# Score matmuls of a gated linear recurrence: from blocks of 64 keys in one or two column groups to blocks of 32 keys in four

## The chip, the cores and the metric

The kernel runs on one core of a Trainium2 chip as one program. The metric is the device time of one execution in microseconds (us), the median over several runs. Engines are named as in the profile: PE is TensorE (its matmuls) and PEld the loading of weights into TensorE; DVE is VectorE, ACT is ScalarE, POOL is GpSimd, SP is the engine whose queue issues nearly all DMAs.

## The reference

The program is a two-layer network in float32 on 1024 tokens of width 1024: sliding-window attention, a squared-relu MLP, a gated linear recurrence (HGRN2), and a second MLP. The change touches the recurrence alone. For each of its 8 heads (key and value width 128), in 16 chunks of 64 tokens, it computes

```python
b = jnp.cumsum(lc, axis=2)                       # lc = log of the forget gate
o_inter = jnp.einsum('bhtd,bhde->bhte', qc * jnp.exp(b), state)
diff = b[:, :, :, None, :] - b[:, :, None, :, :]
decay = jnp.exp(jnp.where(causal[None, None, :, :, None], diff, -jnp.inf))
scores = jnp.einsum('bhtd,bhtsd,bhsd->bhts', qc, decay, kc)
o_intra = jnp.einsum('bhts,bhse->bhte', scores, vc)
b_last = b[:, :, -1]
new_state = jnp.exp(b_last)[..., None] * state + jnp.einsum(
    'bhsd,bhse->bhde', kc * jnp.exp(b_last[:, :, None, :] - b), vc)
```

A score of a query at time t and a key at time s is thus a sum over 128 dimensions of q, k and the product of the forget gates between s and t. That product depends on the dimension, so the scores are not one matrix product.

## The kernel before, in words

**Layout.** Activations lie transposed: 128 dimensions on the partitions, 512 tokens (one half, `hf`) along a tile; `NH = 2` halves, `BPH = 4` blocks of 128 tokens in each. The kernel works the recurrence in blocks of 128 tokens.

**Scores by doubling.** For each head, `recurrence` builds the decayed queries and keys by doubling the span (`double`, H = 1, 2, 4 ... 64): at level `lg` (H = 2 to the power lg) the tokens are seen in spans of 2H; the queries of the later half of each span carry the gates' product back to the middle of the span, and the keys of the earlier half carry it on to there, so a plain matrix product gives the scores between the two halves of each span. `level` makes these products. Its weights are the keys, its moving columns the later halves of the queries alone (`later`), so half as many columns as keys. Of each product only the entries of the right spans are kept: `merge` copies them from PSUM into `scores` through a mask (COPY_PREDICATED on DVE). The diagonal comes from one more set of products (`own`), which DVE multiplies by `diag`.

**What is issued per head.** A chunk is `CH = 64` tokens; there are 16 in the two halves. Keys of even chunks write PSUM rows 0 to 63, keys of odd chunks rows 64 to 127; the PSUM rows are the column group of the TensorE array, so neighbours in the order go to different groups. `own` and the six levels 0 to 5 have 16 matmuls each; the products between the two chunks of a block of 128 tokens (`cross`) are 8 matmuls, all in rows 0 to 63. That makes 120 matmuls per head. They are float32, and the profile has two weight loads and two MATMUL records for each. They stand in two stretches: `own` and levels 0 to 2 first, levels 3 to 5 and `cross` some 16 us later, after further doublings.

**From scores to outputs.** ACT copies `scores` and `cross` into the 128 by 128 lower triangle `s` of every block (three copies for each half, 64 partitions by 256), POOL clears the upper corner, and later matmuls multiply `s` by the values and add the state's part.

**What sets the order.** No loop order is final. Each operation is recorded with a price per engine (`mm`, `tt`, `copy` and so on); `Schedule.order` simulates the engines with these prices in four passes of forward list scheduling and backward due times, and the best pass sets the order on every engine for the entire program. The recurrence of head e is woven into the gate projections of head e + 1 (`interleave` in `hgrn`): big matmuls of 128 by 512 against weights that ACT and DVE split into a high and a low part (`weight_split`: tiles `wh`, `wl`). All operations are issued by one helper, so the profile shows them all at one line; tiles tell them apart: `p` and `q` are PSUM banks (4 each), `t` and `a` float32 tiles, `wr` raw weights, `m` short-lived tiles, `c` constants, `d` DRAM. The score matmuls write `q`.

**Prices of the planner.** A score matmul is priced at 64 x 2.06 / 2.4 + 4 = 58.9 ns, one of `cross` at 64 x 3.9 / 2.4 + 4 = 108 ns; these numbers set an order, they are not measurements of this run.

Of the kernel before, what the change touches and what calls it, by code (L numbers as in the profile page):

```python
# [22 lines left out]
TH = T // NH  # L23
# [11 lines left out]
BPH = NBLK // NH  # L35
# [4 lines left out]
PI_DOWN = float(np.float32(3.1415925))  # L40
BUFS = {"a": 60, "t": 18, "m": 6, "sm": 8, "wr": 6, "wh": 5, "wl": 5, "p": 4, "q": 4}
CH = 64
LEVELS = 6
HOMES = "aaaaaaaaaaaa"
K_SPANS = ((-1, 3), (2, 6), (5, 8))

# [91 lines left out]
HALF = {"ACT": 125.0, "DVE": 105.0}  # L138
# [240 lines left out]
class Net:  # L379
# [1011 lines left out]
    def hgrn_constants(self):  # L1391
        bounds = self.const((P, 2 * KT))
        self.dma(bounds, self.io["lb"], 4 * P * 2 * KT)
        l0, l1 = (bounds[:, i * KT : i * KT + KT] for i in range(2))
        top, e0, e1, lb = (self.const((P, KT)) for _ in range(4))
        self.tt("DVE", top, l0, l1, ALU.max, KT)
        for e, l in ((e0, l0), (e1, l1)):
            self.tt("DVE", e, l, top, ALU.subtract, KT)
            self.act(e, e, AF.Exp, KT)
        self.tt("DVE", lb, e0, e1, ALU.add, KT)  # L1400
        self.op("DVE", self.nc.vector.reciprocal, [lb], [lb], 100, lb, lb)
        self.tt("DVE", e0, e0, lb, ALU.mult, KT)
        self.tt("DVE", e1, e1, lb, ALU.mult, KT)
        self.tt("DVE", lb, e0, e1, ALU.add, KT)
        self.tt("DVE", lb, lb, e0, ALU.subtract, KT)
        self.f_mul, self.f_add = self.const((P, KT)), self.const((P, KT))
        self.ts("DVE", self.f_mul, lb, -0.5, 0.5, ALU.mult, ALU.add, KT)
        self.tt("DVE", self.f_add, self.f_mul, lb, ALU.add, KT)
        nc = self.nc
        si, ti, bits = (self.t(I32, (P, CH)) for _ in range(3))  # L1410
        self.op("Pool", nc.gpsimd.iota, [si], [], 300, si, pattern=[[0, CH]], base=0, channel_multiplier=1)
        self.op("Pool", nc.gpsimd.iota, [ti], [], 300, ti, pattern=[[1, CH]], base=0, channel_multiplier=0)
        self.ts("DVE", si, si, CH - 1, None, ALU.bitwise_and, None, CH)
        self.tt("DVE", bits, si, ti, ALU.bitwise_xor, CH)
        self.diag = self.const((P, CH))
        self.ts("DVE", self.diag, bits, 0, None, ALU.is_equal, None, CH)
        self.level_mask = []
        for lg in range(LEVELS):
            mask, later = self.const((P, CH), I32), self.t(I32, (P, CH))
            self.ts("DVE", mask, bits, lg, None, ALU.logical_shift_right, None, CH)  # L1420
            self.ts("DVE", mask, mask, 1, None, ALU.is_equal, None, CH)
            self.ts("DVE", later, ti, 1 << lg, None, ALU.bitwise_and, None, CH)
            self.ts("DVE", later, later, 0, None, ALU.is_gt, None, CH)
            self.tt("DVE", mask, mask, later, ALU.mult, CH)
            self.level_mask.append(mask)

    def put_by(self, views):
# [85 lines left out]
    def recurrence(self, e, gates, totals, out):  # L1513

        nc = self.nc
        NC = NH * BPH
        chunk = lambda z, j: z[:, j * CH : j * CH + CH]
        scores = self.t(F32, (P, NC, CH))
        tots, tot = [self.t(tag="m") for _ in range(NH)], [g[1] for g in gates]
        qs, ks = ([g[i] for g in gates] for i in (0, 2))  # L1520
        later = lambda z, H: z.rearrange("p (n a h) -> p n a h", a=2, h=H)[:, :, 1]
        at = 0

        def level(lg, part, qs, ks, late):
            H = 1 << lg
            for hf, (q, k) in enumerate(zip(qs, ks)):
                for c in range(BPH):
                    for b in range(2):
                        rows, j = slice(b * CH, b * CH + CH), 2 * c + b
                        self.mm(part[rows, hf * BPH + c], chunk(k, j), later(chunk(q, j), H), True, True, CH, 2.06, "columns", late)  # L1530

        def merge(lg, part):
            H = 1 << lg
            n = CH // (2 * H)
            mask = later(self.level_mask[lg], H).unsqueeze(1).to_broadcast([P, NC, n, H])
            target = scores.rearrange("p c (n a h) -> p c n a h", a=2, h=H)[:, :, :, 1]
            part = part.rearrange("p c (n h) -> p c n h", n=n)
            self.op("DVE", nc.vector.copy_predicated, [target], [mask, part], 70 + TH // 2 * 1.04, target, mask, part)

        def part_of(bank, i):  # L1540
            return bank[:, i * TH // 2 : (i + 1) * TH // 2].rearrange("p (c t) -> p c t", c=NC)

        first = [self.t() for _ in range(NH)]
        for z, (q, f, k, g, v) in zip(first, gates):
# [2 lines left out]
        at, tot, q1, k1 = self.double(1, first, ks, tot, tots, at, self.t)  # L1547
        yield
        at, tot, q2, k2 = self.double(2, q1, k1, tot, tots, at, self.t)
        yield  # L1550
        own, low, two = (self.psum("q") for _ in range(3))
        own = own.rearrange("p (c t) -> p c t", c=NC)
        late = qs + ks + first + q1 + k1 + q2 + k2
        for hf, (q, k) in enumerate(zip(qs, ks)):
            for c in range(BPH):
                for b in range(2):
                    rows, j = slice(b * CH, b * CH + CH), 2 * c + b
                    self.mm(own[rows, hf * BPH + c], chunk(k, j), chunk(q, j), True, True, CH, 2.06, "columns", late)
        level(0, part_of(low, 0), first, ks, late)
        level(1, part_of(low, 1), q1, k1, late)  # L1560
        level(2, part_of(two, 0), q2, k2, late)
        self.tt("DVE", scores, own, self.diag.unsqueeze(1).to_broadcast([P, NC, CH]), ALU.mult)
        merge(0, part_of(low, 0))
        merge(1, part_of(low, 1))
        merge(2, part_of(two, 0))
        qs, ks = q2, k2
        yield
        at, tot, qs, ks = self.double(4, qs, ks, tot, tots, at)
        yield
        at, tot, q4, k4 = self.double(8, qs, ks, tot, tots, at, self.t)  # L1570
        yield
        at, tot, q5, k5 = self.double(16, q4, k4, tot, tots, at, self.a)
        yield
        at, tot, q6, k6 = self.double(32, q5, k5, tot, tots, at, self.t)
        yield
        low, top, cross = (self.psum("q") for _ in range(3))
        late = qs + ks + q4 + k4 + q5 + k5 + q6 + k6
        level(3, part_of(low, 0), qs, ks, late)
        level(4, part_of(low, 1), q4, k4, late)
        level(5, part_of(top, 0), q5, k5, late)  # L1580
        cross = cross[:CH].rearrange("p (c t) -> p c t", c=NC)
        for hf, (q, k) in enumerate(zip(q6, k6)):
# [20 lines left out]
        for hf, (q, k) in enumerate(zip(qs, ks)):  # L1603
            v, g = back[2 * hf : 2 * hf + 2]
            s = weights[hf]
# [7 lines left out]
            up = self.psum("q").rearrange("p (c e) -> p c e", c=BPH)  # L1613
# [317 lines left out]
```

## Time and profile before

| what | value |
| --- | --- |
| median of 3 runs (range) | 2050.99 us (2050.57 to 2051.39) |
| span of the profiled execution | 2048.9 us; the page shows no other time for it |
| PE busy | 2037.5 us, 99% |
| DVE, ACT, POOL busy | 1854.9 us (91%), 1306.6 us (64%), 57.3 us (3%) |
| bytes moved by DMA | 497.19 MB, 243 GB/s on average |
| recurrences, first score load to the last | about 971 to 1359 us into the span, one head every 53 us |

Busy times of an engine count overlapping instructions once. A matmul's record includes a latency of some 0.2 us that overlaps its neighbours, so many small matmuls have a mean far above the time that each adds; what each adds is read from a stretch of them, its length by their count.

### The profile page before, as it was taken

The numbers are of one execution on the slowest core, as the hardware profiler recorded it, in microseconds if no ns is written. First come the engines' busy times: TensorE is split into PE (matmuls) and PEld (weight loads), VectorE is DVE, ScalarE is ACT, GpSimd is POOL, SyncE is SP. The second block draws the span as 40 slices with busy tenths as digits, with TensorE's granted clock in tenths as the row PEclk, the third lists the DMA queues.
The fourth block names the chain that finished last, engine by engine and source line by source line (L and its number), as shares of the span: only waits on it lengthen the run. The fifth ranks groups of instructions, "written<-read, shape, count | busy, mean of one in ns | idle before, by whom it ended". The sixth has DMA issues, their size and how long they took to land.

```text
span 2048.9 us, 36889 instructions
## 1 busy us (share of the span) xinstructions
PE 2037.5 (99%) x12300; PEld 1740.4 (85%) x12300; DVE 1854.9 (91%) x3751; ACT 1306.6 (64%) x2711; POOL 57.3 (3%) x120
## 2 busy tenths in 40 slices
PE   9999999999999999999999999999999999999998
PEld 8878888899998888888888888888889999888887
DVE  8899979899999979889988889999999899997985
ACT  7577976667675544657665556666767677544573
POOL 4030000000000000000000000000000000000000
PEclk9999999999999999999999999999999999999999
DMA  6212378788789977665777788988798788997712
GB/s 227 78 52 73 134 262 270 234 273 287 262 291 312 319 264 255 214 205 198 267 267 267 264 272 286 322 287 301 246 297 293 271 286 285 323 323 238 267 52 83
DMA packets 275407, 497.19 MB, mean 243 GB/s; under 512 B 30992, under 2 KB 36368, under 8 KB 275216
## 3 DMA queue, kind: packets, MB, share of 16 engines
q1 hardware_dynamic: 275072, 494.81, 71.6%
q8 instruction: 97, 1.59, 0.3%
q14 instruction: 94, 0.77, 0.1%
q10 hardware_dynamic: 144, 0.02, 0.0%
HBM read 394.57 MB, written 100.14 MB: 241 GB/s over the span
## 4 chain that ended last, share of the span: by engine, by line
PE 93%; DVE 4%; DMA 1%; issue 1%; ACT 0%; SPq 0%; DVEq 0%
PE p L433 50%; PE q L433 44%; DVE t L433 1%; DVE a L433 1%; DVE wl L433 1%; DMA a<-in_wg 1%; DMA a<-in_x 0%; DVE m L433 0%; DVE sm L433 0%; SPq L433 0%; DMA c<-in_sinks 0%; ACT m L433 0%; ACT a L433 0%; DVE c L433 0%; ACT t L433 0%
## 5 line engine op out<-in xcount | busy, mean ns | idle before, releaser
L433 PE MATMUL p<-a,wh 128*128 128x512 f32 (+1 forms) x2832 | 779.4, 360 | 0.3 <-DVE a L433 0.2
L433 PE MATMUL q<-a,wh 128*128 128x512 f32 x2020 | 625.5, 390 | 0.0
L433 PEld LDWEIGHTS p<-a,wh 128*128 128x128 f32 x2832 | 503.0, 189 | 79.6 <-DVE a L433 1.3
L433 PE MATMUL p<-a,wl 128*128 128x512 f32 (+1 forms) x1416 | 503.5, 358 | 0.4 <-DVE wl L433 0.4
L433 PEld LDWEIGHTS q<-a,wh 128*128 128x128 f32 x2020 | 374.9, 188 | 73.8 <-ACT a L433 0.2
L433 PE MATMUL q<-a,wl 128*128 128x512 f32 x1008 | 392.1, 389 | 0.0
L433 ACT CAST wh<-m 128x512 fp32r<-128x512 f32 (+1 forms) x354 | 213.4, 607 | 195.8 <-PE q L433 100.0
L433 ACT CAST wh<-wr 128x512 fp32r<-128x512 f32 (+1 forms) x324 | 194.9, 604 | 172.5 <-PE p L433 104.6
L433 PEld LDWEIGHTS p<-a,wl 128*128 128x128 f32 x1416 | 266.0, 189 | 38.4 <-DVE wl L433 1.1
L433 DVE TENSOR_TENSOR wl<-m,wh 128x512 fp32r<-128x512 f32 (+1 forms) x354 | 234.4, 668 | 37.5 <-ACT wh L433 31.6
L433 DVE TENSOR_TENSOR a<-t,a 128x512 fp32r<-128x512 f32 (+2 forms) x321 | 211.2, 674 | 18.8 <-PE q L433 7.8
L433 DVE TENSOR_TENSOR wl<-wr,wh 128x512 fp32r<-128x512 f32 (+1 forms) x324 | 214.3, 665 | 15.3 <-ACT wh L433 13.5
L433 DVE TENSOR_TENSOR t<-t,t 128x512 f32<-128x512 f32 (+3 forms) x376 | 218.5, 601 | 9.5 <-ACT t L433 7.1
L433 PEld LDWEIGHTS q<-a,wl 128*128 128x128 f32 x1008 | 189.3, 188 | 39.2
L433 ACT ACTIVATE t<-t 128x512 f32<-128x512 f32 x288 | 179.5, 631 | 58.7 <-DVE t L433 47.6
L433 ACT CAST a<-t 128x512 fp32r<-128x512 f32 (+1 forms) x241 | 143.2, 607 | 24.2 <-DVE t L433 9.5
L433 DVE TENSOR_TENSOR t<-t,p 128x256 f32<-128x256 f32 x288 | 115.9, 414 | 15.0 <-PE p L433 11.2
L433 PE MATMUL p<-wh,a 128*128 128x512 f32 x384 | 125.9, 397 | 0.3 <-DVE a L433 0.3
L433 DVE TENSOR_TENSOR m<-wr,wr 128x512 f32<-128x512 f32 (+1 forms) x184 | 118.8, 648 | 0.3
L433 ACT COPY t<-q 128x512 f32<-128x512 f32 (+2 forms) x174 | 95.7, 556 | 20.6 <-PE q L433 16.1
L433 DVE TENSOR_TENSOR a<-a,a 128x512 fp32r<-128x512 f32 (+2 forms) x151 | 100.8, 679 | 7.7 <-ACT a L433 3.2
L433 ACT CAST a<-a 128x512 fp32r<-128x512 f32 x136 | 82.7, 619 | 25.8 <-DVE a L433 21.8
(135 smaller groups left out, 2535.9 us busy)
## 6 DMA issues: line engine op xcount, KB each, us to landing
t<-d SPq DMA_DIRECT2D x592, 256.0 KB, 4.6
a<-d SPq DMA_DIRECT2D x318, 256.0 KB, 4.2
d<-t SPq DMA_DIRECT2D x290, 256.0 KB, 3.3
wr<-in_down SPq DMA_DIRECT2D x224, 256.0 KB, 4.2
wr<-in_up SPq DMA_DIRECT2D x172, 256.0 KB, 4.3
wr<-in_win SPq DMA_DIRECT2D x68, 256.0 KB, 4.1
d<-a SPq DMA_DIRECT2D x64, 256.0 KB, 3.3
wr<-in_wqkv SPq DMA_DIRECT2D x48, 256.0 KB, 3.0
```

Source lines behind the costliest of these rows:

```text
L433: fn(*[place(a) for a in args], **{k: place(v) for k, v in kw.items()})
```

## The change

The block of keys becomes `QB = 32` tokens. `own` and levels 0 to 4 are made for blocks of 32 keys, whose four column groups (PSUM rows 0, 32, 64, 96) follow each other in the order: 32 matmuls each, with 32 moving columns in `own` and 16 in a level. Level 5 (`top`), the products between the two blocks of 32 of a chunk, becomes 16 matmuls of 32 keys by 32 queries, and is kept whole, with no mask. `cross` becomes 16 matmuls of 32 keys by 64 queries over all four groups. That makes 224 matmuls per head, each again two weight loads and two records.

`scores` holds only the blocks of 32 by 32 on the diagonal, 256 columns where there were 512, so DVE's product with `diag` and its five merges (there were six) work on half the columns. The triangle `s` is assembled from more pieces: for each half 4 copies from `scores`, 4 from `top` and 2 from `cross` on ACT (there were 3), and 3 clears on POOL (there was 1). `own` and levels 0 and 1 share a PSUM bank, as do levels 3 and 4 and `cross`; each stretch takes two banks where it took three. The planner's price is 32 x 0.98 / 2.4 + 4 = 17.1 ns for a score matmul and 30.1 ns for one of `cross`.

```diff
--- before.py
+++ after.py
@@ -40,7 +40,8 @@
 CH = 64
-LEVELS = 6
+QB = 32
+LEVELS = 5
...
@@ -1407,21 +1408,21 @@
-        si, ti, bits = (self.t(I32, (P, CH)) for _ in range(3))
+        si, ti, bits = (self.t(I32, (P, QB)) for _ in range(3))
...
-        self.diag = self.const((P, CH))
+        self.diag = self.const((P, QB))
...
-            mask, later = self.const((P, CH), I32), self.t(I32, (P, CH))
+            mask, later = self.const((P, QB), I32), self.t(I32, (P, QB))
...
@@ -1514,31 +1515,29 @@
 
         nc = self.nc
         NC = NH * BPH
-        chunk = lambda z, j: z[:, j * CH : j * CH + CH]
-        scores = self.t(F32, (P, NC, CH))
+        block = lambda z, j, n=1: z[:, j * QB : (j + n) * QB]
+        scores = self.t()[:, : NC * QB].rearrange("p (c t) -> p c t", c=NC)
         tots, tot = [self.t(tag="m") for _ in range(NH)], [g[1] for g in gates]
         qs, ks = ([g[i] for g in gates] for i in (0, 2))
         later = lambda z, H: z.rearrange("p (n a h) -> p n a h", a=2, h=H)[:, :, 1]
         at = 0
 
-        def level(lg, part, qs, ks, late):
-            H = 1 << lg
+        def level(lg, bank, at, qs, ks, late):
+            n = NC * QB // 2
+            part = bank[:, at * n : at * n + n].rearrange("p (c t) -> p c t", c=NC)
             for hf, (q, k) in enumerate(zip(qs, ks)):
-                for c in range(BPH):
-                    for b in range(2):
-                        rows, j = slice(b * CH, b * CH + CH), 2 * c + b
-                        self.mm(part[rows, hf * BPH + c], chunk(k, j), later(chunk(q, j), H), True, True, CH, 2.06, "columns", late)
+                for j in range(4 * BPH):
+                    rows = slice(j % 4 * QB, j % 4 * QB + QB)
+                    self.mm(part[rows, hf * BPH + j // 4], block(k, j), later(block(q, j), 1 << lg), True, True, QB, 0.98, "columns", late)
+            return part
 
         def merge(lg, part):
             H = 1 << lg
-            n = CH // (2 * H)
+            n = QB // (2 * H)
             mask = later(self.level_mask[lg], H).unsqueeze(1).to_broadcast([P, NC, n, H])
             target = scores.rearrange("p c (n a h) -> p c n a h", a=2, h=H)[:, :, :, 1]
             part = part.rearrange("p c (n h) -> p c n h", n=n)
-            self.op("DVE", nc.vector.copy_predicated, [target], [mask, part], 70 + TH // 2 * 1.04, target, mask, part)
-
-        def part_of(bank, i):
-            return bank[:, i * TH // 2 : (i + 1) * TH // 2].rearrange("p (c t) -> p c t", c=NC)
+            self.op("DVE", nc.vector.copy_predicated, [target], [mask, part], 70 + NC * QB // 2 * 1.04, target, mask, part)
 
         first = [self.t() for _ in range(NH)]
         for z, (q, f, k, g, v) in zip(first, gates):
@@ -1548,21 +1547,17 @@
         yield
         at, tot, q2, k2 = self.double(2, q1, k1, tot, tots, at, self.t)
         yield
-        own, low, two = (self.psum("q") for _ in range(3))
-        own = own.rearrange("p (c t) -> p c t", c=NC)
+        low, two = (self.psum("q") for _ in range(2))
+        own = low[:, : NC * QB].rearrange("p (c t) -> p c t", c=NC)
         late = qs + ks + first + q1 + k1 + q2 + k2
         for hf, (q, k) in enumerate(zip(qs, ks)):
-            for c in range(BPH):
-                for b in range(2):
-                    rows, j = slice(b * CH, b * CH + CH), 2 * c + b
-                    self.mm(own[rows, hf * BPH + c], chunk(k, j), chunk(q, j), True, True, CH, 2.06, "columns", late)
-        level(0, part_of(low, 0), first, ks, late)
-        level(1, part_of(low, 1), q1, k1, late)
-        level(2, part_of(two, 0), q2, k2, late)
-        self.tt("DVE", scores, own, self.diag.unsqueeze(1).to_broadcast([P, NC, CH]), ALU.mult)
-        merge(0, part_of(low, 0))
-        merge(1, part_of(low, 1))
-        merge(2, part_of(two, 0))
+            for j in range(4 * BPH):
+                rows = slice(j % 4 * QB, j % 4 * QB + QB)
+                self.mm(own[rows, hf * BPH + j // 4], block(k, j), block(q, j), True, True, QB, 0.98, "columns", late)
+        parts = [level(0, low, 2, first, ks, late), level(1, low, 3, q1, k1, late), level(2, two, 0, q2, k2, late)]
+        self.tt("DVE", scores, own, self.diag.unsqueeze(1).to_broadcast([P, NC, QB]), ALU.mult, NC * QB)
+        for lg, part in enumerate(parts):
+            merge(lg, part)
         qs, ks = q2, k2
         yield
         at, tot, qs, ks = self.double(4, qs, ks, tot, tots, at)
@@ -1573,27 +1568,36 @@
         yield
         at, tot, q6, k6 = self.double(32, q5, k5, tot, tots, at, self.t)
         yield
-        low, top, cross = (self.psum("q") for _ in range(3))
+        low, two = (self.psum("q") for _ in range(2))
         late = qs + ks + q4 + k4 + q5 + k5 + q6 + k6
-        level(3, part_of(low, 0), qs, ks, late)
-        level(4, part_of(low, 1), q4, k4, late)
-        level(5, part_of(top, 0), q5, k5, late)
-        cross = cross[:CH].rearrange("p (c t) -> p c t", c=NC)
+        parts = [level(3, low, 0, qs, ks, late), level(4, low, 1, q4, k4, late)]
+        top = two[:, : NC * QB // 2].rearrange("p (c t) -> p c t", t=QB)
+        cross = low[:, TH // 2 :].rearrange("p (c t) -> p c t", t=CH)
+        for hf, (q, k) in enumerate(zip(q5, k5)):
+            for j in range(2 * BPH):
+                c, r = j // 2, (j % 2 * 2 + j // 2 % 2) * QB
+                self.mm(top[r : r + QB, (hf * BPH + c) // 2], block(k, 2 * j), block(q, 2 * j + 1), True, True, QB, 0.98, "columns", late)
         for hf, (q, k) in enumerate(zip(q6, k6)):
-            for c in range(BPH):
-                self.mm(cross[:, hf * BPH + c], chunk(k, 2 * c), chunk(q, 2 * c + 1), True, True, CH, 3.9, "columns", late)
-        merge(3, part_of(low, 0))
-        merge(4, part_of(low, 1))
-        merge(5, part_of(top, 0))
+            for j in range(2 * BPH):
+                c, r = j // 2, (j // 2 % 2 * 2 + j % 2) * QB
+                self.mm(cross[r : r + QB, (hf * BPH + c) // 2], block(k, 4 * c + j % 2), block(q, 4 * c + 2, 2), True, True, CH, 0.98,
+                        "columns", late)
+        for lg, part in enumerate(parts):
+            merge(3 + lg, part)
         qs, ks = q6, k6
         yield
         weights = []
         for hf in range(NH):
             s, c = self.t(F32, (P, BPH, 2, CH)), slice(hf * BPH, hf * BPH + BPH)
-            self.memset(s[CH:, :, 0].only(0), 0.0, "Pool")
-            self.copy(s[:CH, :, 0].only(1), scores[:CH, c], 4 * CH, more=HALF["ACT"])
-            self.copy(s[CH:, :, 1].only(2), scores[CH:, c], 4 * CH, more=HALF["ACT"])
-            self.copy(s[:CH, :, 1].only(3), cross[:, c], 4 * CH, more=HALF["ACT"])
+            pair = slice(hf * BPH // 2, hf * BPH // 2 + BPH // 2)
+            self.memset(s[CH:, :, 0].only("low"), 0.0, "Pool")
+            for b in range(2):
+                up, down = (slice(b * CH + i * QB, b * CH + i * QB + QB) for i in range(2))
+                self.memset(s[down, :, b, :QB].only(f"z{b}"), 0.0, "Pool")
+                for i, rows in enumerate((up, down)):
+                    self.copy(s[rows, :, b, i * QB : i * QB + QB].only(f"d{b}{i}"), scores[rows, c], BPH * QB, more=HALF["ACT"])
+                    self.copy(s[up, i::2, b, QB:].only(f"t{b}{i}"), top[rows, pair], BPH * QB // 2, more=HALF["ACT"])
+                self.copy(s[:CH, b::2, 1].only(f"c{b}"), cross[b * CH : b * CH + CH, pair], BPH * CH // 2, more=HALF["ACT"])
             weights.append(s)
         at, tot, qs, ks = self.double(CH, qs, ks, tot, tots, at)
         back = [self.back(gates[hf][i]) for hf in range(NH) for i in (4, 3)]
```

On PE, at the first stretch of the fifth head, before (an entry `x8` is one half's eight matmuls of one product; the tiles `t` are the decayed keys and queries, `p` and `wh`/`wl` belong to the next head's projections):

```order
L433 MATMUL p_15013<-a_11167,wl_14764 128x512
L433 MATMUL q_15048<-t_14222,t_14768 64x64 x8
L433 MATMUL q_15048<-t_14306,t_14867 64x64 x8
L433 MATMUL q_15072<-t_14891,t_14768 64x32 x8
L433 MATMUL q_15072<-t_14902,t_14867 64x32 x8
L433 MATMUL q_15072<-t_14931,t_14795 64x32 x8
L433 MATMUL q_15072<-t_14962,t_14944 64x32 x8
L433 MATMUL q_15110<-t_14975,t_14950 64x32 x8
L433 MATMUL q_15110<-t_14987,t_14955 64x32 x8
L433 MATMUL p_14886<-a_11520,wh_14876 128x512
```

and now, at the same row of the order:

```order
L434 MATMUL p_15478<-a_11145,wl_15237 128x512
L434 MATMUL q_15514<-t_14570,t_15235 32x32 x16
L434 MATMUL q_15514<-t_14652,t_15338 32x32 x16
L434 MATMUL q_15514<-t_15365,t_15235 32x16 x16
L434 MATMUL q_15514<-t_15357,t_15338 32x16 x16
L434 MATMUL q_15514<-t_15391,t_15261 32x16 x16
L434 MATMUL q_15514<-t_15415,t_15429 32x16 x16
L434 MATMUL q_15622<-t_15451,t_15401 32x16 x16
L434 MATMUL q_15622<-t_15465,t_15437 32x16 x16
L434 MATMUL p_15351<-a_11513,wh_15424 128x512
```

The stretch stands at the same place, in one piece between the same kinds of big matmuls; each product has twice the matmuls on blocks of half the keys, and the diagonal's products now write the bank of levels 0 and 1.

On ACT, where the fifth head's triangles are assembled (`q_15391` is `cross`, `t_15093` is `scores`, `t_15406` and `t_15412` are the two halves' triangles; the CAST behind is a weight's high part for a projection), before:

```order
L433 COPY t_15347<-p_15231 128x512
L433 COPY t_15406<-t_15093 64x4x64 x2
L433 COPY t_15406<-q_15391 64x4x64
L433 COPY t_15412<-t_15093 64x4x64 x2
L433 COPY t_15412<-q_15391 64x4x64
L433 CAST wh_15438<-m_15302 128x512
```

and now (`q_15930` is `top`, `q_15855` the bank with `cross`, `t_15639` is `scores`):

```order
L434 COPY t_15878<-p_15760 128x512
L434 COPY t_15970<-q_15930 32x2x32 x2
L434 COPY t_15970<-q_15855 64x2x64
L434 COPY t_15970<-q_15930 32x2x32 x2
L434 COPY t_15970<-q_15855 64x2x64
L434 COPY t_15970<-t_15639 32x4x32 x4
L434 COPY t_15986<-q_15930 32x2x32 x4
L434 COPY t_15986<-t_15639 32x4x32 x4
L434 COPY t_15986<-q_15855 64x2x64 x2
L434 CAST wh_16042<-m_15836 128x512
```

Twenty copies stand in one run where six stood, ahead of the same cast; SP issues as many DMAs as before.

More of the change, by code (lines that the diff above doesn't have):

```diff
@@ L1409, in hgrn_constants @@
         nc = self.nc
-        si, ti, bits = (self.t(I32, (P, CH)) for _ in range(3))
[L1411 to L1414, printed above, removed]
-        self.diag = self.const((P, CH))
-        self.ts("DVE", self.diag, bits, 0, None, ALU.is_equal, None, CH)
+        si, ti, bits = (self.t(I32, (P, QB)) for _ in range(3))
+        self.op("Pool", nc.gpsimd.iota, [si], [], 300, si, pattern=[[0, QB]], base=0, channel_multiplier=1)
+        self.op("Pool", nc.gpsimd.iota, [ti], [], 300, ti, pattern=[[1, QB]], base=0, channel_multiplier=0)
+        self.ts("DVE", si, si, QB - 1, None, ALU.bitwise_and, None, QB)
+        self.tt("DVE", bits, si, ti, ALU.bitwise_xor, QB)
+        self.diag = self.const((P, QB))
+        self.ts("DVE", self.diag, bits, 0, None, ALU.is_equal, None, QB)
         self.level_mask = []
         for lg in range(LEVELS):
-            mask, later = self.const((P, CH), I32), self.t(I32, (P, CH))
[L1420 to L1424, printed above, removed]
+            mask, later = self.const((P, QB), I32), self.t(I32, (P, QB))
+            self.ts("DVE", mask, bits, lg, None, ALU.logical_shift_right, None, QB)
+            self.ts("DVE", mask, mask, 1, None, ALU.is_equal, None, QB)
+            self.ts("DVE", later, ti, 1 << lg, None, ALU.bitwise_and, None, QB)
+            self.ts("DVE", later, later, 0, None, ALU.is_gt, None, QB)
+            self.tt("DVE", mask, mask, later, ALU.mult, QB)
             self.level_mask.append(mask)
```

## The prediction

> **What bounds the kernel now.** I read the page first: the busy shares, and the chain that ended last.
>
> ```profile
> PE 2037.5 (99%) x12300; PEld 1740.4 (85%) x12300; DVE 1854.9 (91%) x3751; ACT 1306.6 (64%) x2711; POOL 57.3 (3%) x120
> PE 93%; DVE 4%; DMA 1%; issue 1%; ACT 0%; SPq 0%; DVEq 0%
> ```
>
> PE is never idle for long, and the chain lies on it. A busy PE is no proof of a bound, since records overlap, so I took the stretches of the recurrences next: all eight heads together, and the last stretch alone, which is the densest one for DVE. Columns: the stretch, its length, busy us of PE, PEld, DVE, ACT, POOL with counts, granted clock, DMA share, GB/s.
>
> ```profile
> core 0: us, PE busy (x) PEld busy (x) DVE busy (x) ACT busy (x) POOL busy (x), PEclk, DMA share, GB/s
> 960.00:1400.00 440.00, 439.71 (x3820) 375.69 (x3819) 406.23 (x885) 272.26 (x606) 7.74 (x18) 1.00 0.82 280
> 1331.00:1400.00 69.00, 68.71 (x552) 58.50 (x551) 66.60 (x139) 48.29 (x103) 0.61 (x2) 1.00 0.82 284
> ```
>
> PE has 0.29 us of idle time in 440. DVE is busy 92.3% there, 96.5% in the last 69 us. The clock is full and the DMA engines have a fifth of their time left. The chain of the same part, and what it is made of in one head:
>
> ```profile
> by line: PE p L433 68.8%; PE q L433 27.2%; DMA a<-in_wg 2.5%; DVE t L433 0.6%; DVE wl L433 0.5%; DVE a L433 0.3%; issue 0.1%; SPq L433 0.0%; DVEq L433 0.0%
> 1130.70 3.86 PE q L433 x128
> 1134.55 16.54 PE p L433 x72
> 1151.10 3.88 PE q L433 x112
> ```
>
> The two score stretches, 3.86 and 3.88 us of every 53, are whole pieces of the chain. Time taken from them shortens the chain, as long as DVE keeps up.
>
> **What sets the length of a score stretch.** The weight loads of the first head's score matmuls, in order of time (start, length, group, count), then a run of full-width float32 matmuls, a run of matmuls with one moving column (its matmul records), and the mean record of each kind:
>
> ```profile
> 971.49 3.81 PEld L433 LDWEIGHTS q<-t,t 128*64 128x64 f32 x128 [0.35 <-PE p L433]
> 991.89 1.95 PEld L433 LDWEIGHTS q<-t,t 128*64 128x64 f32 x64 [0.35 <-issue]
> 993.75 1.02 PEld L433 LDWEIGHTS q<-a,a 128*64 128x64 f32 x32
> 994.69 1.01 PEld L433 LDWEIGHTS q<-t,t 128*64 128x64 f32 x16
> 1002.91 0.97 PEld L433 LDWEIGHTS q<-t,t 128*128 128x128 f32 x8 [0.26 <-ACT t L433]
> 2010.57 1.84 PE L433 MATMUL q<-c,t 128*128 128x1 f32 x16
> L433 PEld LDWEIGHTS q<-t,t 128*64 128x64 f32 x1664 | 54.2, 138 | 5.6 <-issue 4.6 <-PE p L433 0.7 <-DVE t L433 0.4
> L433 PEld LDWEIGHTS q<-t,t 128*128 128x128 f32 x240 | 33.4, 191 | 1.2 <-ACT t L433 0.3
> L433 PE MATMUL q<-c,t 128*128 128x1 f32 x96 | 11.6, 236 | 0.0
> ```
>
> `cross` (x16), all in one column group: (1.01 - 0.138) / 15 = 58.1 ns from load to load. The first stretch (x128), alternating between two groups: (3.81 - 0.138) / 127 = 28.9 ns, which is 63 steps of 58.3 ns with two loads in each. So a group takes a new load every 58 ns, and two groups do so side by side. The moving columns do not set this: levels have 32 and `cross` 64, both at 58; and one moving column behind 128 weight columns still costs (1.84 - 0.236) / 15 = 107 ns, nearly the (0.97 - 0.191) / 7 = 111.3 ns of 128 moving columns. The weight columns set it: 128 cost 111.3 ns, 64 cost 58.3, that is 0.83 ns per column and 5 ns on top.
>
> Per head now: 64 steps of 58.3 ns, 48 of 58.5 (x64 and x32: 991.89 to 994.69) and 16 of 58.1 make 3.73 + 2.81 + 0.93 = 7.47 us.
>
> **The change on PE.** 224 matmuls, 448 loads of 32 columns, four groups in turn. No load of 32 columns and no run over four groups is in the trace; the cost of 448 is bounded by these rows:
>
> - best: a load shrinks in proportion (29.1 ns) and four groups run side by side: 112 x 29.1 = 3.26 us;
> - the straight line through the two measured widths, 58.3 - 32 x 0.83 = 31.8 ns, four groups: 112 x 31.8 = 3.56 us;
> - no shrinking, four groups: 112 x 58.3 = 6.53 us;
> - shrinking, but only two groups at a time: 224 x 31.8 = 7.12 us;
> - worst: 28.9 ns between any two starts is what the engine needs, whatever the group: 448 x 28.9 = 12.95 us.
>
> I take 3.56. Both facts behind it are in the rows: two groups halve the spacing of one, and half the width takes nearly half the time. In each step of 31.8 ns even the 64 moving columns of `cross` should disappear, as they do now in 58. Gain: 7.47 - 3.56 = 3.91 us per head, **31.3 us for eight**; at most 33.7.
>
> A rule of the Trainium skill speaks against this. "TensorE: Matmul & The Clock Gate", section "Wait — 56ns, not 53.3ns?", has a floor of about 25 ns from start to start however few columns move; taken for the whole engine it would make 448 x 25 = 11.2 us a head. The same page of the Trainium skill, in "Part 3: Packing small matmuls — row/col tiling", has matmuls in different tiles start some 4 ns apart, which would leave the 3.56 us. The trace contradicts neither: its mean spacing of 28.9 ns lies above both, so the floor is a rival below.
>
> **The other engines.** From the groups of the six middle heads (1013 to 1331 us; x6 is one per head, x36 six), and POOL's of 960 to 1400 us:
>
> ```profile
> L433 DVE TENSOR_TENSOR t<-q,c 128x512 f32<-128x512 f32 x6 | 4.1, 680 | 0.0
> L433 DVE COPY_PREDICATED t<-c,q 128x256 f32<-128x256 int32 x36 | 19.3, 536 | 2.9 <-PE q L433 1.9
> L433 DVE TENSOR_TENSOR t<-t,m 128x256 f32<-128x256 f32 x96 | 35.5, 420 | 0.0
> L433 ACT COPY t<-t 64x256 f32<-64x256 f32 x24 | 9.7, 405 | 14.5 <-DVE t L433 14.2
> L433 ACT COPY t<-q 64x256 f32<-64x256 f32 x12 | 4.0, 366 | 0.2
> L433 ACT COPY m<-q 128x128 f32<-128x128 f32 x6 | 1.6, 266 | 6.2 <-PE q L433 6.2
> L433 POOL MEMSET t<- 64x256 f32 x16 | 4.7, 306 | 459.5 <-PE q L433 188.1 <-ACT wh L433 138.7 <-DMA a<-d 105.1
> ```
>
> DVE: the product with `diag` at 680 ns becomes one of 256 columns, 420; six merges at 536 become five of half the width. 256 columns less cost 260 ns less in the product, so 128 less are worth 130: 406 each (between 268, half, and 536, no change). Before 0.68 + 6 x 0.536 = 3.90 us, after 0.42 + 5 x 0.406 = 2.45: 1.45 us per head and 11.6 in all off DVE (from 6 to 17 by the two ends). It is worth nothing by itself, since PE hides it, but DVE needs it: 406.2 - 11.6 = 394.6 us in 440 - 31 = 409 is 96.5%, exactly the share of the last 69 us, where PE lost 0.29 us of 69. At that rate 409 us lose 1.7; I take 2 us off the gain.
>
> ACT: 4 x 405 + 2 x 366 = 2.35 us per head become 8 copies of 128 columns from SBUF, 8 of 64 and 4 of 128 from PSUM. By 266 ns for 128 columns from PSUM, 39 more from SBUF (405 against 366) and about 213 for 64 columns (266 less 64 columns at the 0.78 ns between 128 and 256): 8 x 0.305 + 8 x 0.213 + 4 x 0.266 = 5.2 us. That is 2.9 us more per head on an engine that is busy 272 of 440 us, some 72% afterwards. These copies stand in one run; behind them waits a cast of weights (`wh`), for which PE waits in the end.
>
> ```profile
> ACT wh L433 <- PE p L433: 29.1, 39, 1.6
> ACT t L433 <- DVE t L433: 78.3, 56, 3.8
> ```
>
> In 960 to 1375 us those casts were themselves held by PE 39 times: the five `wh` buffers were full. A delay of 2.9 us is covered by that stock, since one buffer serves twelve matmuls and a run of 72 takes 16.54 us: 12 last 2.8 us. Without that cover it would cost up to 2.9 us per head, 23 in all. I price it at nothing.
>
> POOL clears 6 pieces per head in place of 2, at most 4 x 306 = 1.2 us on an idle engine, nothing. SP issues the same DMAs; their share rises from 0.82 to 0.82 x 440 / 409 = 0.88. The planner orders the whole program anew; PE is 99% busy everywhere, so I give its shifts 3 us either way and no sign.
>
> **Sum.** 31.3 - 2 = 29.3 us. Against the profiled execution 2048.9 - 29.3 = 2019.6 us of span; the median of the runs is 2.1 us above that span, so **2022 us**. A difference of over 0.2%, 4 us, is what a measurement of this kernel can tell from no change.
>
> **The rivals.**
>
> *B, the groups do not pay as they did from one to two.* Two at a time: gain 0.35 x 8 = 2.8 us, 2048. No shorter load: 0.94 x 8 = 7.5 us, 2043. For it: nothing of either kind is in the trace. Against it: two points on a straight line, and two groups that hardly disturb each other (58.3 against 58.1 ns).
>
> *C, DVE takes over.* If it cannot be used above its present 92.3%, the part lasts 394.6 / 0.923 = 427.5 us: a gain of 12.5, **2038**. Against it: the last 69 us with 96.5%.
>
> *D, slower: one floor for all starts on PE.* The place is PE's queue in the two stretches; the price is the spacing s of starts: 448 x s against 7.47 us. It decides from s = 16.7 ns on. At today's mean of 28.9 it costs 5.48 us per head, 2051 + 43.8 = **2095**; where s is between, in between. For it: no row shows a run of starts closer than 28.9 ns on average. Against it: that spacing is accounted for in full by a group's 58 ns, and one group alone has 58 where the engine's limit would have let it have 28.9. By the 25 ns of the Trainium skill it would be 2051 + 29.8 = 2081.
>
> *E, no change*, because a stretch's end waits for something else: DVE's product that comes later with a shared bank, or the copies. The chain shows no such wait; within 4 us of 2051.
>
> **How the numbers follow.** Forecast 0.66 (its own range 2014 to 2032: the best load, up to 23 us more on ACT partly uncovered, 3 us of order), B 0.08, C 0.10, D 0.13, E 0.03. Faster: forecast, C and over half of B, 0.81; same: 0.06; slower: 0.13. The range leaves out D and the edges, 2014 to 2047.
>
> **What would show it.** Right: a run of 448 loads of 128x32 with 7 to 9 ns per load and score stretches near 2.0 and 1.5 us in the chain; heads 49 us apart; PE still without idle time, DVE at 96%. Loads at 14 to 16 ns mean B, 17 ns and more D; idle PE before `wl` or `wh` means C, or that the casts behind the copies come late. Wrong altogether if stretches shorten and the heads' distance does not.

## The result, and the profile after

The changed kernel takes 2086.47 us (median of 4 runs, 2083.27 to 2087.6) against 2050.78 us: a ratio of 1.0171, with a 95% interval of 1.0157 to 1.0186. It is 35.7 us slower, where 29 us faster was forecast. Its profiled execution has a span of 2081.1 us, 32.2 more than before.

The page of the changed kernel: the engines' busy time with their counts of instructions, the traffic of instructions (packets, MB, share), and the group that holds most of the score matmuls, with 240 others (count, busy us, mean ns of one, idle us before them).

```profile
PE 2031.6 (98%) x13964; PEld 1725.9 (83%) x13964; DVE 1839.7 (88%) x3738; ACT 1329.1 (64%) x2823; POOL 61.3 (3%) x152
...
q8 instruction: 110, 1.80, 0.3%
...
L434 PE MATMUL q<-t,t 128*32 128x16 f32 (+2 forms) x3568 | 78.8, 199 | 36.2 <-issue 35.6
```

In the part before, PE had 0.29 us of idle time in 440. Now it stands still for 36 us in front of the score matmuls alone, and the releaser is named "issue": the engine waited for nothing that the profile shows, no other engine and no DMA of the program. All waits of PE from 960 to 1400 us (us in total, times, longest):

```profile
PE q L434 <- issue: 36.7, 11, 4.8
PE q L434 <- ACT t L434: 0.7, 1, 0.7
```

Where these waits lie is seen in the weight loads of the first heads, in order of time (start, length, group, count, and in brackets the idle time before):

```profile
970.01 1.51 PEld L434 LDWEIGHTS q<-t,t 128*32 128x32 f32 x158 [0.35 <-PE p L434]
975.73 1.50 PEld L434 LDWEIGHTS q<-t,t 128*32 128x32 f32 x98 [4.21 <-issue]
...
1026.18 2.32 PEld L434 LDWEIGHTS q<-t,t 128*32 128x32 f32 x245 [0.35 <-issue]
1031.39 0.20 PEld L434 LDWEIGHTS q<-t,t 128*32 128x32 f32 x11 [2.89 <-issue]
...
1055.74 0.61 PEld L434 LDWEIGHTS q<-t,t 128*32 128x32 f32 x20 [4.29 <-issue]
...
1371.48 2.38 PEld L434 LDWEIGHTS q<-t,t 128*32 128x32 f32 x256 [0.35 <-issue]
```

Two things stand in these rows. The loads themselves go nearly as fast as hoped: 256 in 2.38 us in the eighth head, with no wait between them, 9 ns each. And stretches are cut, after a different count of loads each time (158 in the first head, 245 in the second, its second stretch 20 before its end), in the rows shown by 2.9 to 4.3 us of nothing. None of the eight first stretches is spared: in the eighth all loads run through, and PE's matmuls wait 2.19 us before the last of them. A dependence of the program would hardly move from head to head like that.

The count between waits gives the pattern away. Stretches of the changed kernel from the end of one wait to the end of the next; PEld's count is in brackets:

```profile
975.73:1031.39 55.66, 52.87 (x761) 44.58 (x762) 47.35 (x113) 35.68 (x88) 4.53 (x8) 0.96 0.71 243
1031.39:1055.74 24.35, 20.23 (x256) 16.46 (x255) 18.13 (x38) 11.53 (x25) 1.41 (x6) 0.93 0.65 220
1055.74:1091.48 35.74, 32.81 (x380) 27.81 (x380) 27.38 (x65) 22.38 (x58) 0.00 (x0) 0.95 0.74 250
1091.48:1144.52 53.04, 49.61 (x635) 41.76 (x635) 45.01 (x100) 34.55 (x85) 1.41 (x6) 1.00 0.79 269
```

762, 255, 380 and 635 loads are 6, 2, 3 and 5 times 127, or one off. A load and its matmul are two instructions, so 127 pairs are 254, and some semaphore instructions of PE come in between: the waits lie multiples of 256 instructions apart. The page says the same in another way: PE has 1664 more loads and as many more matmuls, 3328 instructions, and the instruction queue q8 moved 110 packets where the page of before has 97. 3328 / 13 = 256. (In the experiments below, e2 with 3840 more instructions of PE than before has 112 packets, e3 and e6 with no more have 97.) PE's program reaches it in blocks of 256 instructions, and the two score stretches of a head, with 512 and 384 instructions in some 2 us each, use them up faster than they come.

The trace shows the blocks themselves, too: it has the time of every packet of q8, 16384 bytes each. When all instructions of PE are counted, those for semaphores included, the eleven waits end at the same place of the count, at instruction 193 or 194 of 256, and each ends 1.3 to 1.7 us after a packet of q8 has landed. The first: the packet moves from 973.43 to 974.43 us, and PE goes on at 975.73. At the other 32 such places from 960 to 1440 us the packet had landed at least 1.4 us before, and PE did not wait.

The wait has a second price. The first cut again, as stretches of time (the third number from the end is the granted clock):

```profile
971.50:975.70 4.20, 0.13 (x14) 0.03 (x2) 1.16 (x2) 0.00 (x0) 0.00 (x0) 0.78 0.70 263
975.70:977.30 1.60, 1.56 (x99) 1.53 (x99) 0.33 (x1) 0.00 (x0) 0.00 (x0) 0.50 0.05 14
...
979.00:981.00 2.00, 2.00 (x7) 1.53 (x6) 0.95 (x4) 0.00 (x0) 0.00 (x0) 0.59 0.03 8
...
960.00:1430.00 470.00, 432.48 (x5477) 362.14 (x5476) 388.18 (x872) 294.32 (x715) 14.44 (x50) 0.96 0.76 260
```

The clock falls to half within the wait and is at 0.59 on average still from 979 to 981 us, so the half clock outlasts the wait by some 5 us. Over 470 us the mean is 0.96, so 0.04 x 470 = 19 us of full clock are missing.

### The profile page after: what moved, and what is told of

Its sections match the earlier page's. It is cut to its first block, busy times and chain, and to the rows that moved or that the text cites. A ratio compares the mean times of both kernels' runs of the same rounds, so it can differ in the third digit from the quotient of the medians.

```text
span 2081.1 us, 40285 instructions
## 1 busy us (share of the span) xinstructions
PE 2031.6 (98%) x13964; PEld 1725.9 (83%) x13964; DVE 1839.7 (88%) x3738; ACT 1329.1 (64%) x2823; POOL 61.3 (3%) x152
## 4 chain that ended last, share of the span: by engine, by line
PE 95%; issue 2%; DVE 2%; ACT 0%; DMA 0%; SPq 0%; DVEq 0%; ACTq 0%
PE p L434 53%; PE q L434 42%; DVE a L434 1%; DVE t L434 0%; DVE wl L434 0%; DVE m L434 0%; DMA a<-in_x 0%; ACT t L434 0%; DMA t<-d 0%; ACT m L434 0%; ACT wh L434 0%; DVE sm L434 0%; ACT a L434 0%; SPq L434 0%; ACT sm L434 0%
## 5 line engine op out<-in xcount | busy, mean ns | idle before, releaser
L434 PE MATMUL p<-a,wh 128*128 128x512 f32 (+1 forms) x2832 | 791.6, 364 | 0.4 <-DVE a L434 0.2
L434 PEld LDWEIGHTS p<-a,wh 128*128 128x128 f32 x2832 | 511.1, 191 | 83.0 <-DVE a L434 0.9
L434 PE MATMUL p<-a,wl 128*128 128x512 f32 (+1 forms) x1416 | 510.1, 363 | 0.7 <-DVE wl L434 0.7
L434 ACT COPY t<-q 128x512 f32<-128x512 f32 (+2 forms) x254 | 111.5, 442 | 57.9 <-PE q L434 39.0
L434 PE MATMUL q<-t,t 128*32 128x16 f32 (+2 forms) x3568 | 78.8, 199 | 36.2 <-issue 35.6
```

The lines of the kernel that those rows point to most:

```text
L434: fn(*[place(a) for a in args], **{k: place(v) for k, v in kw.items()})
```

## Experiments

Three theories were set against each other. **Theory 1**: the supply of PE's instructions, in blocks of 256. **Theory 2**: the array, or its queue, cannot sustain matmuls over four column groups. **Theory 3**: a wait for another engine or a PSUM bank that the profile calls issue.

### Same matmuls, four stretches (e1_four_stretches)

The order of `recurrence` is changed so that `own` and level 0, levels 1 and 2, levels 3 and 4, and `top` with `cross` each form a stretch:

```diff
-        low, two = (self.psum("q") for _ in range(2))
+        low = self.psum("q")
...
-        late = qs + ks + first + q1 + k1 + q2 + k2
+        late = qs + ks + first
...
+        merge(0, part)
+        at, tot, q1, k1 = self.double(1, first, ks, tot, tots, at, self.t)
+        yield
+        at, tot, q2, k2 = self.double(2, q1, k1, tot, tots, at, self.t)
+        yield
+        two = self.psum("q")
+        late = q1 + k1 + q2 + k2
+        parts = [level(1, two, 0, q1, k1, late), level(2, two, 1, q2, k2, late)]
```

> The changed kernel with its score matmuls in four stretches of 112 to 128 weight loads (own and level 0; levels 1 and 2; levels 3 and 4; top and cross), 24 to 48 big matmuls apart, in place of two of 256 and 192. Theory 1 (instruction supply: PE gets its instructions in blocks of 256, 128 load-and-matmul pairs, and needs some 4 to 6 us for the next block; the two stretches of the change use 2 and 1.5 blocks in 2 us each): crossings of blocks lie 5.6 us and more apart, most of the 36.7 us of PE waiting for 'issue' goes, under 10 us remain, and the time falls to 2022 to 2035 us. Theory 2 (the array or its queue cannot sustain matmuls over four column groups): the same work in the same groups stalls as before, 2080 us and more. Theory 3 (a wait for DVE, ACT or a PSUM bank that the profile calls issue): the waits stay, one per stretch, 2070 us and more.

Measured: 2040.15 us, 0.995 of the time before (0.9933 to 0.9966). The waits of PE in 960 to 1400 us:

```profile
PE q L434 <- issue: 4.5, 3, 2.5
PE p L434 <- issue: 0.7, 1, 0.7
```

5.2 us where there were 36.7, with the same matmuls in the same groups. The longest that is left stands in the eighth head, where the planner put the first two stretches into one of 256 loads. Theory 3 falls in the form of one wait per stretch, and theory 2 in the form that narrow matmuls stall as such. A limit on the length of a run of them is not excluded here, nor a bank that only the two long stretches wait for; the order of the banks was changed too. The time is some 5 us above theory 1's range.

### Wide matmuls, each issued twice (e2_wide_twice)

The kernel before, with twice the instructions in the stretches and no narrow matmul (each product is written twice with the same result):

```diff
-            for hf, (q, k) in enumerate(zip(qs, ks)):
+            for hf, (q, k) in 2 * list(enumerate(zip(qs, ks))):
```

in `level`, and the same for `own` and `cross`.

> The kernel before, 64 keys in two groups, with every score matmul issued twice (the second writes the same result): 256 and 224 weight loads per head at 29 ns, so a block of 256 instructions lasts 3.7 us. The added PE work alone is 7.47 x 8 = 60 us, 2111 us. Theory 1: blocks are crossed 3.7 us apart inside a stretch, which is shorter than the 4.2 to 5.7 us that a block took in the changed kernel's stalls, so there are waits of 0.5 to 2 us at one or two crossings per head, 8 to 25 us of issue in all against 4.6 before, and the time is 2118 to 2140 us. Theory 2 (four narrow groups are at fault): no waits, 4 to 6 us of issue, 2108 to 2114 us. Theory 3: no waits either, since banks and other engines are as before.

Measured: 2128.79 us, 1.038 of the time before (1.0359 to 1.04). The loads of the first stretch of the first head:

```profile
971.20 4.80 PEld L433 LDWEIGHTS q<-t,t 128*64 128x64 f32 x161 [0.35 <-PE p L433]
977.15 2.88 PEld L433 LDWEIGHTS q<-t,t 128*64 128x64 f32 x95 [1.16 <-issue]
```

And PE's waits for issue in 960 to 1440 us:

```profile
PE q L433 <- issue: 8.6, 7, 2.1
```

Matmuls with 64 columns in two groups wait for issue too, when two blocks of instructions are wanted one behind the other, 128 loads at 28.9 ns or 3.7 us each; before, the same matmuls once each had no such wait. (The 4.6 us before that the expectation names are idle time of the loads; PE itself had no wait for issue.) Theory 2 falls in the form that four narrow groups are at fault. A limit on the length of a run is not excluded by e2, whose runs are twice as long; it does not fit the changed kernel, where runs of 256 loads stopped after 158, 245, 205, 165, 252, 203 and 168 of them. The waits are shorter (8.6 / 7 = 1.2 us each against 36.7 / 11 = 3.3) and fewer than one per head, as befits a block that lasts three times as long. Of the 78 us, 60 are the added matmuls by the spacings of the prediction; the waits are 8.6. Most of the other 10 is the clock: the trace has half clock behind three of the waits, for 17.1 us together, which is up to 8.5 us of work.

### The price of splitting (e3_wide_four_stretches)

The kernel before, with the edit of e1 on its wide matmuls; of the later stretches:

```diff
+        low = self.psum("q")
+        late = qs + ks + q4 + k4
+        level(3, part_of(low, 0), qs, ks, late)
+        level(4, part_of(low, 1), q4, k4, late)
+        merge(3, part_of(low, 0))
+        merge(4, part_of(low, 1))
         at, tot, q5, k5 = self.double(16, q4, k4, tot, tots, at, self.a)
...
-        late = qs + ks + q4 + k4 + q5 + k5 + q6 + k6
```

> The kernel before with its score matmuls in the same four stretches as e1: the price of the splitting by itself. Theories 1 and 2 alike: two more changes between column and whole mode per head at some 0.35 to 0.5 us each, at most 8 us: 2051 to 2059 us, no waits for issue. Theory 3: no change of waits either.

Measured: 2057.55 us, 1.0032 (1.0021 to 1.0044), with no wait of PE for issue: 6.7 us for 15 more stretches (the planner joined two in the eighth head), 0.44 each.

### Four stretches, evenly apart (e4_even)

As e1, with empty steps between the stretches and one step of the recurrence for each step of the projections (`before, 14, 14`):

```diff
         at, tot, q2, k2 = self.double(2, q1, k1, tot, tots, at, self.t)
         yield
+        yield
         two = self.psum("q")
...
-            interleave(self.gates(e, streamed if e else x, self.rs, r, got, [None] * 2 if e else begun), before, 14, 12)
+            interleave(self.gates(e, streamed if e else x, self.rs, r, got, [None] * 2 if e else begun), before, 14, 14)
```

> As e1, but with the four stretches 36 big matmuls (8.3 us) apart each. Theory 1: a block of 256 instructions now never lasts less than some 8 us, so no wait for issue remains above the 5 us of the kernel before, the granted clock is 1.00 throughout, and the time is 2020 to 2030 us, faster than both kernels. Theories 2 and 3: waits stay, 2070 us and more.

Measured: 2039.64 us, 0.9946 (0.9931 to 0.9961): faster than both kernels, but not to be told from e1, and 10 us above the range. Beside e3 it has the same four stretches; it differs in the width of the matmuls, and in how far apart the stretches stand. The first loads of the first two heads of e3:

```profile
966.16 1.95 PEld L433 LDWEIGHTS q<-t,t 128*64 128x64 f32 x64 [0.35 <-issue]
...
1019.87 1.95 PEld L433 LDWEIGHTS q<-t,t 128*64 128x64 f32 x64 [0.35 <-issue]
```

The same of e4, with the second stretch of the first head, and two stretches of the sixth:

```profile
965.41 1.19 PEld L434 LDWEIGHTS q<-t,t 128*32 128x32 f32 x128 [0.35 <-PE p L434]
...
975.02 1.20 PEld L434 LDWEIGHTS q<-t,t 128*32 128x32 f32 x128 [0.35 <-PE p L434]
...
1015.97 1.19 PEld L434 LDWEIGHTS q<-t,t 128*32 128x32 f32 x128 [0.35 <-PE p L434]
...
1224.47 1.19 PEld L434 LDWEIGHTS q<-t,t 128*32 128x32 f32 x128 [0.35 <-issue]
...
1226.81 0.83 PEld L434 LDWEIGHTS q<-t,t 128*32 128x32 f32 x82 [0.37 <-issue]
1231.14 0.52 PEld L434 LDWEIGHTS q<-t,t 128*32 128x32 f32 x46 [3.50 <-issue]
```

And e4's waits of PE for issue in 960 to 1400 us:

```profile
PE q L434 <- issue: 4.1, 3, 3.4
PE p L434 <- issue: 1.9, 1, 1.9
```

From the first head to the second 53.71 us become 50.56, so this head is 3.15 us shorter with narrow matmuls, which would be 25.2 in eight; the next three are shorter by 3.32, 3.46 and 3.37. The whole runs differ by 17.9 us. A part of the rest has its place in the loads of the sixth head: the planner put two stretches 2.3 us apart, where the first head has 9.6, and there a wait of 3.5 us is back. All waits, 6.0 us, and the half clock behind them, which the trace has twice for 3.41 us (up to 3.4 us of work), are enough for the 7.3 us between 25.2 and 17.9; how the two share them was not divided.

### The blocks moved against the stretches (e5_shifted)

16 more matmuls, 64 instructions, at the head of the very first stretch:

```diff
+        for _ in range(16 if e == 0 else 0):
+            self.mm(own[:QB, 0], block(ks[0], 0), block(qs[0], 0), True, True, QB, 0.98, "columns", late)
```

> The changed kernel with 16 more matmuls (64 instructions, 32 weight loads; the first own matmul repeated) at the head of the first head's first stretch; every order is otherwise the same. Theory 1 (a wait falls on the second crossing of a 256-instruction block inside a stretch): in program positions all crossings stay, so relative to the stretches they move 32 loads earlier. In the changed kernel the waits stood after 158 loads of head 1's first stretch, 245 of head 2's, 205 of head 3's, 175 of head 4's, and after 172 loads of head 2's second stretch; now after about 158 again (the added loads come first), 214, 174 and 134; head 1's second stretch, which had no wait, gets one after about 179 loads, head 2's second after 140, and the total stays within 10 us of the change, 2076 to 2097 us. Theory 2 (the array stalls on four groups) and any cause tied to a place of the program (a bank, an operand): the waits of heads 2 to 8 stand where they stood.

Measured: 2094.35 us (one run). The loads of the first heads:

```profile
970.32 2.18 PEld L434 LDWEIGHTS q<-t,t 128*32 128x32 f32 x159 [0.35 <-PE p L434]
974.80 1.91 PEld L434 LDWEIGHTS q<-t,t 128*32 128x32 f32 x126 [2.29 <-issue]
978.75 0.18 PEld L434 LDWEIGHTS q<-t,t 128*32 128x32 f32 x3 [2.04 <-issue]
...
1005.05 0.26 PEld L434 LDWEIGHTS q<-t,t 128*32 128x32 f32 x12 [4.98 <-issue]
...
1041.03 0.50 PEld L434 LDWEIGHTS q<-t,t 128*32 128x32 f32 x43 [3.32 <-issue]
```

The waits moved with the count of instructions, not with the work: after 159 loads in the first head and once more 126 loads later, 256 - 43 = 213 in the second (245 before the shift), a new one 12 loads before the end of the first head's second stretch, which had none. Banks and operands are those of the changed kernel, so theory 3 falls here in every form that ties a wait to its place in the program. One expectation was a miss: the fourth head's first stretch ran through with no wait at load 134, and the wait came at the following crossing from one block to the next, among the big matmuls behind it. The packet for the crossing at load 134 had landed 1.4 us before PE came to it.

### One part alone: cross over two groups (e6_cross_two_groups)

The kernel before, its 8 `cross` matmuls per head alternating between PSUM rows 0 to 63 and 64 to 127; the copy behind them becomes two, one for each half:

```diff
-                self.mm(cross[:, hf * BPH + c], chunk(k, 2 * c), chunk(q, 2 * c + 1), True, True, CH, 3.9, "columns", late)
+                r = c % 2 * CH
+                self.mm(cross[r : r + CH, (hf * BPH + c) // 2], chunk(k, 2 * c), chunk(q, 2 * c + 1), True, True, CH, 2.06, "columns", late)
```

> The kernel before, 64 keys, with the 8 cross matmuls of a head alternating between the two column groups (rows 0 to 63 and 64 to 127), and two ACT copies of 128 columns per half in place of one of 256: one part of the change alone, which adds no instruction on PE. If a column group takes a load every 58 ns and groups run side by side, the 16 loads take 0.47 us in place of 0.93, 3.7 us in all: 2046 to 2049 us, and no wait for issue. If groups do not overlap there, 2051 us.

Measured: 2048.1 us, 0.9988 (0.9978 to 0.9997). The loads of `cross`:

```profile
994.61 0.55 PEld L433 LDWEIGHTS q<-t,t 128*64 128x64 f32 x16
```

(0.55 - 0.138) / 15 = 27.5 ns where one group had 58.1: groups run side by side, with no instruction added and no wait. The gain is 2.4 us of the 3.7 that the loads save; where the other 1.3 went stays open.

## Why the prediction was wrong, point by point

**The bound was read rightly.** PE bounded the part, and the score stretches lay whole on the chain: their waits show in the time.

**The price of the loads was nearly right.** The forecast was 448 loads in 112 steps of 31.8 ns, 3.56 us per head. Without waits the first stretch takes 2.38 us for 256 loads. The second stretch of the third head, with 128 loads of level 3 and 4, 32 of `top` and 32 of `cross`:

```profile
1108.60 1.22 PEld L434 LDWEIGHTS q<-t,t 128*32 128x32 f32 x128 [0.35 <-issue]
1109.73 0.39 PEld L434 LDWEIGHTS q<-a,a 128*32 128x32 f32 x32
1110.02 0.52 PEld L434 LDWEIGHTS q<-t,t 128*32 128x32 f32 x32
```

And the group of all of them but those of `top` (busy us, mean ns of one):

```profile
L434 PEld LDWEIGHTS q<-t,t 128*32 128x32 f32 x3328 | 36.0, 114 | 40.0 <-issue 39.3 <-PE p L434 0.7
```

With 0.114 us for a load itself, that is 8.9, 8.7, 8.9 and 13.1 ns each: 2.28 + 1.11 + 0.28 + 0.42 = 4.1 us. The gain of 3.91 us a head was 3.4; e4 against e3 shows 3.15 to 3.46 in the first four heads. The sentence that even the 64 moving columns of `cross` should disappear was wrong: they cost 13 ns against 9.

**The step that failed is the sum on PE.** It took a stretch to last as long as its loads, and no term of it, and no rival, counted what PE must be given: 896 instructions in 3.6 us, 4 ns each, where the kernel before had 480 in 7.5 us. What the runs showed in its place is a supply in blocks of 256, for which PE waited eleven times, 36.7 us in all. The rows that would have warned stood in the page of before: 97 packets of instructions, and 1.59 MB of them, which is 16 KB each. The same packets and the count of instructions give a block of 256. The trace of before also has the time of each packet: some 1.0 us to move, and from 960 to 1440 us the packet of the next block started up to 3.6 us after PE had entered the block ahead of it. That is slower than the some 1.1 us in which 128 narrow matmuls use up a block. What that trace could not show is a wait, since no packet there landed less than 3.2 us before it was needed.

**The account.** 31.3 us of gain were priced, the span grew by 32.2: a gap of 63.5. The waits are 36.7 us, the missing clock up to 19 (a part of it falls into the waits and costs nothing twice), the loads 0.54 x 8 = 4. These make up to 60; the rest of some 4 us is not resolved. The 2 us that the forecast took off for DVE did not show: the waits of PE name no DVE.

**The rivals.** D had the sign and not the mechanism. It was a floor for every start on PE, deciding from 16.7 ns; loads start 9 ns apart, below it, and e4 gains. The 25 ns of the Trainium skill that stood beside it ("TensorE: Matmul & The Clock Gate", section "Wait — 56ns, not 53.3ns?") do not hold for matmuls in different column groups: 9 ns here, for the loads and for the matmul records alike. B fell with the same rows: four groups run side by side. C, DVE taking over, did not come: no wait for DVE stands among those of PE.

**The other engines were priced well.** Groups of the changed kernel in 960 to 1400 us:

```profile
L434 ACT COPY t<-t 32x128 f32<-32x128 f32 x64 | 18.9, 296 | 0.9 <-DVE t L434 0.2
...
L434 DVE COPY_PREDICATED t<-c,q 128x128 f32<-128x128 int32 x40 | 14.0, 350 | 10.6 <-PE q L434 10.4
...
L434 ACT COPY t<-q 32x64 f32<-32x64 f32 x64 | 13.0, 203 | 11.4 <-PE q L434 10.5
...
L434 ACT COPY t<-q 64x128 f32<-64x128 f32 x32 | 8.3, 261 | 12.2 <-DVE t L434 11.8
```

Copies of 296, 203 and 261 ns were put at 305, 213 and 266, merges of 350 at 406. That the twenty copies cost nothing fits e4, whose first four heads gain 3.15 to 3.46 us where the loads save 3.4.

**The signs named** were half right: loads at 7 to 9 ns did come (8.9), heads 49 us apart did not. The sign given for "wrong altogether", shorter stretches with no shorter heads, is what happened in kind; the heads became longer.

## What to carry to other kernels

Many small instructions have a supply as well as a duration: count the instructions of a stretch, divide by 256, and ask how long each block lasts. Here a second block wanted within 1.3 us made PE wait 11 times in 13 in the changed kernel, within 3.7 us it did in places (e2), and a single crossing in a stretch (before, e3) did not. Work that is short and dense in instructions pays when it is dealt out among long instructions, even at 0.44 us for each further stretch; the same matmuls that cost 36 us in two stretches gain 11 us in four.

## What the runs showed of the hardware

**Blocks of instructions.** PE's instructions come in blocks of 256, and a stretch that needs a second block soon after the first waited up to 4.8 us in the changed kernel. The Trainium skill has the block size ("Runtime: NRT & Kernel Launch", section "Instruction fetch mechanics": 16 KiB, 256 instructions, the next block fetched while the present one runs), and the trace agrees with the size; its remark that crossing a block is mostly hidden holds for the kernel before and not here. Some second crossings passed without a wait (the third head's second stretch in the changed kernel, the fourth head's first in e5): there the packet had landed 3.1 and 1.4 us before. In all eight traces taken together, the loads stood still for over 0.9 us at 39 of these crossings, each time until 1.2 to 1.7 us after the packet had landed. A packet takes some 1.0 us to move, and its start lies anywhere from 5 us before to 7 us after PE enters the block ahead of it. What sets that start, the DMA traffic beside it among others, was not tried.

**The clock.** A wait of 4.2 us was followed by half clock for about 5 us. Shorter ones can do it too, but need not: in e2 the wait of 1.16 us shown above left the clock at 1.00 in the 2.8 us behind it, and a wait between 1374 and 1376 us brought it to 0.59 in the 4 us behind. The length of the wait does not decide it: another of 1.17 us in e2, up to 1285.98 us, was followed by a granted clock of 0.51 from 1287 to 1294 us, and the one of 3.03 us that ends at 1091.48 us in the changed kernel by 1.00 over the next 53 us (fourth row of the stretches between waits). From 960 to 1440 us every spell of half clock in these traces lasts 3.41, 6.83 or 10.24 us, one, two or three times the same length. What decides was not tried.

```profile
977.20:980.00 2.80, 2.80 (x95) 2.80 (x95) 1.65 (x3) 0.00 (x0) 0.00 (x0) 1.00 0.53 183
1374.00:1376.00 2.00, 0.36 (x10) 0.36 (x12) 0.25 (x1) 0.00 (x0) 0.00 (x0) 0.96 0.71 248
1376.00:1380.00 4.00, 4.00 (x55) 3.93 (x52) 2.08 (x5) 0.81 (x2) 0.00 (x0) 0.59 0.94 325
```

e4's first head, with narrow stretches and no wait, kept the full clock, so the lower clock goes with the wait and not with the narrow matmul:

```profile
965.00:1015.00 50.00, 50.00 (x675) 41.54 (x674) 47.39 (x117) 35.04 (x88) 2.92 (x7) 1.00 0.81 273
```
